# Second embedding's products inside the last expert, its gate's first chunk loaded ahead

## The chip, the core and the metric

The kernel runs on one core of a Trainium2 chip. The number is the device time of one launch in microseconds, the median of three runs. Five engines work side by side, each with its own queue that is worked off in order: PE (TensorE, matrix products), DVE (VectorE), ACT (ScalarE), POOL (GpSimd) and SP, which here issues the DMA transfers of the weights. They wait for one another through semaphores.

## What is computed

Two transformer blocks follow each other on 256 tokens of 1024 channels. The first block has two layers: a differential attention with a short convolution and a dense SwiGLU, then a gated convolution mixer with a mixture of experts (top 2 of 8). Each layer ends with a gated embedding, which is what the change is about. The second block (two layers of four attention mixers with an adaptive norm) only matters by its first product, which takes the output of the first block. Cut to what the change touches:

```python
def moe_swiglu(h, router_w, w1, w3, w2):
    logits = jnp.einsum('nd,de->ne', xt, router_w)
    top_val, top_idx = lax.top_k(logits, TOP_K)            # 2 of 8 experts per token
    gates = jax.nn.softmax(top_val, axis=-1)
    ...                                                    # rows sorted by expert
    return (jax.nn.silu(xb @ w1[e]) * (xb @ w3[e])) @ w2[e]   # summed with gates

for i in range(DEPTH):                                     # DEPTH = 2
    ...                                                    # mixer of the layer
    h = h + swiglu(rms_norm(h, ln_ffn[i]), ...)            # i = 0
    h = h + moe_swiglu(rms_norm(h, ln_ffn[i]), ...)        # i = 1
    gate = jax.nn.sigmoid(rms_norm(h, ln_ple[i]) @ ple_gate[i])   # 1024 x 1024
    h = h + gate * (p[i] @ ple_proj[i])                    # p[i]: 256 x 256
```

The product `p[i] @ ple_proj[i]` doesn't depend on `h`; the gate does.

## The kernel before

**Layout.** `h` stays in SBUF as `hT`, 128 partitions by eight groups of 128 channels by 256 tokens. Products of fp32 numbers are made of three faster ones: each operand is split into `hi` and `lo` (`xhi`, `xlo` for the activations, `pThi`, `pTlo` for the embedding), and hi by hi, hi by lo and lo by hi are added up in PSUM. ACT makes `hi`, then DVE makes `lo`, half a chunk at a time.

**Weights.** All weights come in one stream of chunks of 1 MB in the order of `stream()` (line 77); a chunk is two halves, so `raw3230` is half 0 of chunk 323. SP issues them (line 310) as buffers come free, `pump()` (351) and `get()` (358) decide when a chunk is split and handed out, and at most `look` split chunks are kept ahead (`may_split()`, 344). The first three experts are split like the rest. The last five are "plain": their chunks are used as fp32 without a split, for fewer tokens each, and need neither ACT nor DVE. Two more pairs of raw buffers (`more_raw`, 2106) are open during part of the first block; `i_raw2` bounds the chunks that may use them.

**Order.** A scheduler sets the order on each engine from the order of the program and from pools and priorities; the lists below are its result.

**The gated embedding.** `ple(l)` (810) loads `pT[l]` into `pt`, splits it, makes the products `pps` of the embedding (`ple_proj`, 797: 48 matmuls, copied by ACT into `pp`), and then runs over four chunks of the gate's weights: product `pg` (48 matmuls each), scaled by the norm's factor into `sg`, a sigmoid on ACT, times `pp`, added to `hT`. The norm's factor comes from squares of `hT` (ACT), their sums (POOL, DVE), `ssq` on PE, `rqt` on ACT, small operations on DVE, `rsp` on PE and `nr` on ACT. With each finished pair of groups the next norm's input (`xhi`, `xlo`) is made. It runs twice, after the dense SwiGLU (l = 0) and after the experts (l = 1).

**The end of the experts.** For each of the last five experts `up` makes `H` (line 1434), ACT and DVE gate it into `mg`, `gTp` transposes it, `down` makes `Ys` (1497), and `combine_plain` (1524) scales `Ys` on ACT into `ys`, spreads it to the tokens with a selection matrix (`sc` on PE) and adds it to `hT` on DVE, which also starts `xhi` and `xlo` for the embedding. In `stream()` the last expert's down chunks come first, then `ple_proj` of layer 1 (chunk 330 before the change), then four gate chunks, then `c0` of the second block. `cw1k`, `pt` and other small tables are loaded by the ACT queue.

**The router.** `slots` (1307) makes the selection matrices `S` from the tokens' places; those of the plain experts are six DVE operations (line 1317) among the others.

## Time and profile before

| | us |
|---|---|
| median of 3 runs | 1873.13 |
| lowest, highest | 1872.68, 1876.75 |
| profiled execution | 1875.38 |
| its span | 1873.6 |

PE is the busiest engine; the first three experts keep it busy without a gap, the last five are fed by DMA at its full rate, and the gated embeddings lie on both sides of the experts and of the mixer before them. Times in the rows below are from the span's start. A row of a timeline has start and duration in us, the engine, the line of the kernel, the operation, output and inputs with their shape, how many instructions are taken together (x16), and in brackets how long the engine had stood idle before and what it waited for.

### The profile page before, as it was taken

How to read it: one execution, taken by the hardware profiler on the slowest of the kernel's cores; microseconds unless marked ns; L12 is line 12 of the kernel's file. 1: busy time of each engine (PE TensorE's matmuls, PEld its weight loads, DVE VectorE, ACT ScalarE, POOL GpSimd, SP SyncE). 2: the span in 40 equal slices, each digit the busy share in tenths (PEclk: the TensorE clock that was granted, in tenths of full speed). 3: DMA queues.
4: the chain of work that ended last, by engine and by line, in shares of the span. 5: the costliest groups of instructions: out<-in, count | busy, mean ns of one | idle time of the engine just before them, and what ended most of it. 6: DMA issues, size and time to landing. Idle time of an engine off the chain costs nothing.

```text
span 1873.6 us, 31611 instructions
## 1 busy us (share of the span) xinstructions
PE 1768.3 (94%) x11889; PEld 1428.9 (76%) x11889; DVE 1176.8 (63%) x2150; ACT 909.2 (49%) x1428; POOL 53.0 (3%) x93
## 2 busy tenths in 40 slices
PE   7999999999999999899898888999999999999998
PEld 7989999997888888333232223887899998889997
DVE  7888888687899988101000011886888877666554
ACT  6754435666787866000000002666555456666553
POOL 1000000000000000000000000200000000000000
PEclk9999999998999999999999999999999999999999
DMA  8479886575899989999999999443588864326651
GB/s 308 144 261 315 309 308 218 185 246 210 297 361 330 368 299 326 376 413 412 413 412 413 412 413 383 163 155 106 209 307 303 314 215 138 113 69 204 190 185 53
DMA packets 138544, 508.55 MB, mean 271 GB/s; under 512 B 18192, under 2 KB 18832, under 8 KB 137872
## 3 DMA queue, kind: packets, MB, share of 16 engines
q1 hardware_dynamic: 132480, 496.92, 73.0%
q10 hardware_dynamic: 5904, 9.53, 1.6%
q8 instruction: 96, 1.57, 0.3%
q14 instruction: 64, 0.52, 0.1%
HBM read 505.34 MB, written 1.05 MB: 270 GB/s over the span
## 4 chain that ended last, share of the span: by engine, by line
PE 31%; DMA 22%; DVE 4%; ACT 2%; issue 1%; SPq 0%; DVEq 0%; ACTq 0%
DMA raw<-in_moe_dram 19%; PE y L632 8%; PE up L406 7%; PE zp L406 5%; DMA adaw<-in_ada_dram 2%; PE H L1434 2%; PE S L1839 2%; DVE lo L326 1%; PE op L406 1%; PE pTp L1045 1%; PE cmh L1946 1%; PE oT L1873 1%; ACT hi L325 1%; DVE adacc L865 1%; PE op L431 1%
## 5 line engine op out<-in xcount | busy, mean ns | idle before, releaser
L326 DVE TENSOR_TENSOR lo<-raw,hi 128x1024 fp32r<-128x1024 f32 x516 | 621.8, 1223 | 131.5 <-ACT hi L325 130.0
L325 ACT ACTIVATE hi<-raw 128x1024 fp32r<-128x1024 f32 x516 | 530.9, 1054 | 185.6 <-PE H L1417 38.2
L1434 PE MATMUL H<-raw,xs 128*64 128x512 f32 (+1 forms) x960 | 229.7, 567 | 39.3 <-DMA raw<-in_moe_dram 32.7
L1434 PEld LDWEIGHTS H<-raw,xs 128*64 128x64 f32 x960 | 75.1, 137 | 182.7 <-issue 97.8
L1444 DVE SCALAR_TENSOR_TENSOR mg<-H,gs,mg 128x512 f32<-128x512 f32 (+3 forms) x38 | 26.3, 692 | 290.1 <-PE H L1434 198.7
L632 PE MATMUL y<-ghi,hi 128*128 128x256 f32 x688 | 193.6, 283 | 3.9 <-ACT ghi L377 3.7
L632 PE MATMUL y<-ghi,lo 128*128 128x256 f32 x688 | 194.0, 282 | 2.0 <-DVE lo L326 2.0
L632 PE MATMUL y<-glo,hi 128*128 128x256 f32 x688 | 194.0, 282 | 1.9 <-DVE glo L378 1.9
L1417 PE MATMUL H<-hi,xg 128*128 128x512 f32 (+1 forms) x576 | 178.1, 382 | 0.0
L1443 ACT ACTIVATE mg<-H,gs 128x512 f32<-128x512 f32 (+3 forms) x38 | 24.2, 636 | 307.0 <-PE H L1434 306.9
L865 DVE SCALAR_TENSOR_TENSOR adacc<-adaw,cact,adacc 128x768 f32<-128x768 f32 x126 | 130.9, 1039 | 47.7 <-DMA adaw<-in_ada_dram 46.0
L406 PE MATMUL up<-xhi,hi 128*128 128x258 f32 x480 | 136.3, 284 | 0.2 <-ACT hi L325 0.2
L406 PE MATMUL up<-xhi,lo 128*128 128x258 f32 x480 | 135.6, 283 | 0.0
L406 PE MATMUL up<-xlo,hi 128*128 128x258 f32 x480 | 135.4, 282 | 0.0
L632 PEld LDWEIGHTS y<-ghi,hi 128*128 128x128 f32 x688 | 129.9, 189 | 5.0 <-ACT ghi L377 4.9
L632 PEld LDWEIGHTS y<-glo,hi 128*128 128x128 f32 x688 | 130.3, 189 | 2.9 <-DVE glo L378 2.9
L632 PEld LDWEIGHTS y<-ghi,lo 128*128 128x128 f32 x688 | 130.2, 189 | 2.6 <-DVE lo L326 2.6
L1497 PE MATMUL Ys<-raw,gts 128*64 128x512 f32 x440 | 119.4, 606 | 8.6 <-DMA raw<-in_moe_dram 7.1
L1417 PEld LDWEIGHTS H<-hi,xg 128*128 128x128 f32 x576 | 105.9, 189 | 20.7
L1417 PE MATMUL H<-lo,xg 128*128 128x512 f32 (+1 forms) x288 | 108.9, 378 | 0.0
L406 PE MATMUL H<-xhi,lo 128*128 128x256 f32 x336 | 94.7, 282 | 0.0
L406 PE MATMUL H<-xhi,hi 128*128 128x256 f32 x336 | 94.3, 281 | 0.0
(604 smaller groups left out, 3820.2 us busy)
## 6 DMA issues: line engine op xcount, KB each, us to landing
raw<-in_moe_dram SPq DMA_DIRECT2D x524, 512.0 KB, 10.0
raw<-in_stream_dram SPq DMA_DIRECT2D x316, 512.0 KB, 4.5
adaw<-in_ada_dram SPq DMA_DIRECT2D x64, 768.0 KB, 6.4
cw1k<-in_cw1k_dram ACTq DMA_DIRECT2D x2, 1024.0 KB, 6.4
cw1v<-in_cw1v_dram ACTq DMA_DIRECT2D x2, 1024.0 KB, 5.5
raw<-in_stream_dram SPq DMA_DIRECT2D x4, 472.0 KB, 4.5
hT<-in_xT_dram SPq DMA_DIRECT2D x4, 256.0 KB, 7.2
raw<-in_stream_dram ACTq DMA_DIRECT2D x2, 512.0 KB, 7.6
```

The costliest lines, as they stand in the source:

```text
L325: self.halved = (nc.scalar.activation(hi, raw, AF.Copy), nc.vector.tensor_sub(lo, raw, hi.bitcast(F32)))
L326: nc.vector.tensor_sub(lo, raw, hi.bitcast(F32)))
L406: nc.tensor.matmul(ps, p[:, k, j:j + m], q[:, k, :], start=start and n == 0, stop=n == 3 * nk - 1, skip_group_check=True)
L431: nc.tensor.matmul(ps, p[:, k, c:c + m[n]], q[:, k, :], start=k == i == 0 and not (n and shared), stop=k == KD - 1 and i == 2, skip_group_ ...
L632: self.nc.tensor.matmul(ps, p[:, k, 128 * dt:128 * dt + 128], q[:, k, :], start=f == 0 and n == 0 and dt % 2 == 0, stop=last and n == 5, s ...
L865: nc.vector.scalar_tensor_tensor(acc, w[:, j], self.cact[:, k:k + 1], acc, op0=OP.mult, op1=OP.add)
L1417: nc.tensor.matmul(ps[:, :n], g[s][:, m // 3], w[:, k], start=m == 0, stop=m == 23, skip_group_check=True)
L1434: nc.tensor.matmul(ps[64 * q:64 * q + 64, :c], g[:, k], x[:, kk], start=k == 0, stop=k == KD - 1, skip_group_check=True)
L1443: nc.scalar.activation(t[z, :c], H[0][z, :c], AF.Silu, scale=gs[z, 1:2])
L1444: nc.vector.scalar_tensor_tensor(t[z, :c], H[1][z, :c], gs[z, 1:2], t[z, :c], op0=OP.mult, op1=OP.mult)
L1497: nc.tensor.matmul(Y[e][64 * q:64 * q + 64], gt[:, kk, 64 * n:64 * n + 64], w[:, k, 512 * q:512 * q + 512], start=key[2] == 0 and kk == 0, ...
L1839: nc.tensor.matmul(S[n][:, c:c + b], q[n][:, a:a + 128], k[n][:, 0:b], start=True, stop=True)
```

## The change

1. `stream()`: the embedding's chunk of layer 1 goes ahead of the last expert's last down chunks, right behind its up chunks, and gate chunk 0 between two of these down chunks. So the embedding's chunk is now chunk 323, gate chunk 0 is chunk 328, and the down chunks end with 331.
2. `ple_in`: loading and splitting `pt` is taken out of `ple`. For layer 0 it is done during the feed-forward's phase, its buffers in a pool around it; for layer 1 when the last expert begins.
3. `ple_proj(1)` is called inside the experts' loop behind the last `up`; `ple_proj(0)` at the start of `ple(0)`.
4. `hush`: from the moment that gate chunk 0 is handed out until the last combination is written down, nothing is split; afterwards `hold` ties later splits to the last `xlo`.
5. `ple(1)` has no phase of its own: it runs in that of the experts, with their `mg` buffers for `sg` and their buffers for one of its squares. The two extra pairs of raw buffers may now serve chunks up to `c0`.
6. The selection matrices of the plain experts take a buffer (`yl`) that is used by a combination before.

```diff
--- before.py
+++ after.py
@@ -113,12 +113,17 @@
     for e, f in moe_steps():
         down = down_keys(*prev) if prev else []
         up = up_keys("m1", e, f) + up_keys("m3", e, f)
-        ch += [(k, shapes[k[0], k[2], k[3]], None) for k in (down + up if (e, f) == (NL, 0) else up + down)]
+        last = (e, f) == moe_steps()[-1]
+        a, b = (down, up) if (e, f) == (NL, 0) else (up, down)
+        ch += [(k, shapes[k[0], k[2], k[3]], None) for k in a]
+        if last:
+            rows(("pple", 1), "ple_proj", (1,), 0)
+        ch += [(k, shapes[k[0], k[2], k[3]], None) for k in b]
         prev = e, f
-    ch += [(k, shapes[k[0], k[2], k[3]], None) for k in down_keys(*prev)]
-    rows(("pple", 1), "ple_proj", (1,), 0)
     for i in range(4):
         cols(("gple", 1, i), "ple_gate", (1,), 256 * i)
+        if i == 0:
+            ch += [(k, shapes[k[0], k[2], k[3]], None) for k in down_keys(*prev)]
     for l in range(2):
         for n, parts in enumerate((
                 [(512, 128), (704, 128)], [(640, 64), (832, 32), (1504, 12), (384, 128)], [(0, 256)],
@@ -266,7 +271,8 @@
         self.i_load = self.i_split = self.i_get = 0
         self.raws, self.parts = {}, {}
         self.homes, self.at_home, self.extra, self.got = [], {}, [], []
-        self.i_raw2 = self.at_key["pple", 1]
+        self.i_raw2 = self.at_key["c0", 0]
+        self.hush = False
 
         self.i_three = self.at_key[down_keys(NL - 1, 5)[-1]]
 
@@ -343,6 +349,8 @@
 
     def may_split(self):
 
+        if self.hush:
+            return False
         if self.i_split not in self.raws or self.plain(self.i_split):
             return self.i_split in self.raws
         return len([i for i in self.parts if not self.plain(i)]) < self.look and \
@@ -494,7 +502,7 @@
         h = self.hT[:, 2 * i:2 * i + 2]
         if self.final is not None:
             return self.out_pair(i, h)
-        self.prep_x(i, h)
+        self.last_x = self.prep_x(i, h)
         self.prep_r(i, h, late=self.rows is not False)
 
     def prep_x(self, i, h):
@@ -513,7 +521,11 @@
         if i == 0:
             self.sqs = []
         for n in range(1 if g2 is None else 2):
-            sq = (self.p_ph if n else self.p_s).tile([128, 2, T], F32, tag=f"sq{n}", name="sq", bufs=3)
+            if n:
+
+                sq = self.p_ph.tile([128, 2, T], F32, tag="gth" if i else "gtl", name="sq", bufs=2)
+            else:
+                sq = self.p_s.tile([128, 2, T], F32, tag="sq0", name="sq", bufs=3)
             if n:
                 for j in range(2):
                     k = 2 * i + j
@@ -659,7 +671,7 @@
         self.p_lo = self.pool("lo", 2 * self.look + 2)
         for pool, tag in ((self.p_hi, "hi"), (self.p_lo, "lo")):
 
-            self.home(pool, self.look + 1, tag, lambda i: self.i_get > self.i_three + 1 and i < self.i_raw2 - 6)
+            self.home(pool, self.look + 1, tag, lambda i: self.i_get > self.i_three + 1 and i < self.at_key["pple", 1] - 6)
             self.homes[-1]["all"] = self.look + 1
         self.p_s = self.pool("small", 2)
         self.p_x = self.pool("x", 4)
@@ -794,11 +806,17 @@
         nc.vector.tensor_sub(t1, u[0], u[1])
         nc.vector.tensor_add(t2, u[2], u[3])
 
+    def ple_in(self, l, tile):
+
+        pt = tile("pt", F32)
+        self.nc.scalar.dma_start(pt, self.a["pT"][l])
+        self.pt = tile("pThi", F32R), tile("pTlo", F32R)
+        yield
+        self.hilo(*self.pt, pt)
+
     def ple_proj(self, l):
-        nc, a = self.nc, self.a
-        pt, hi, lo = self.pt
+        hi, lo = self.pt
         w = self.get(("pple", l))
-        self.hilo(hi, lo, pt)
         pp = self.big("pp", [128, KD, T])
         for i in range(4):
             ps = self.ac("pps", (128, 2, T))
@@ -807,17 +825,13 @@
             self.nc.scalar.activation(pp[:, 2 * i:2 * i + 2], ps, AF.Copy)
         return pp
 
-    def ple(self, l, nxt):
-        nc = self.nc
-        p = self.p_ph
-        pt = p.tile([128, 2, T], F32, name="pt")
-        nc.scalar.dma_start(pt, self.a["pT"][l])
-        self.pt = (pt, p.tile([128, 2, T], F32R, name="pThi"), p.tile([128, 2, T], F32R, name="pTlo"))
-        pp = self.ple_proj(l)
+    def ple(self, l, nxt, pp, w=None, tag="sg"):
+        nc = self.nc
         x = self.nx[0:2]
         for i in range(4):
-            w = self.get(("gple", l, i))
-            if i == 3:
+            if i or w is None:
+                w = self.get(("gple", l, i))
+            if i in (0, 3):
                 self.pump()
             ps = self.mm("pg", (128, 2, T))
             if i:
@@ -827,7 +841,7 @@
                 self.mmT2([ps[:, 0], ps[:, 1]], w, x, (0, 128))
                 self.get_r()
                 self.begin_x(*nxt)
-            sg = self.p_ph.tile([128, 2, T], F32, tag="sg", name="sg", bufs=2)
+            sg = self.p_ph.tile([128, 2, T], F32, tag=tag, name="sg", bufs=2)
             self.scaled(sg, ps)
             nc.scalar.activation(sg, sg, AF.Sigmoid)
             nc.vector.tensor_mul(sg, sg, pp[:, 2 * i:2 * i + 2])
@@ -1305,7 +1319,7 @@
 
 
         def slots(es, off=0, plain=False):
-            S = p.tile([128, 2, len(es), 128], F32R, tag="ST" if off else "Ss" if plain else "S", name="S",
+            S = p.tile([128, 2, len(es), 128], F32R, tag="ST" if off else "yl" if plain else "S", name="S",
                        bufs=2 if off else 1)
             for n, e in enumerate(es):
                 for b in range(2):
@@ -1555,7 +1569,16 @@
                     pass
                 self.moe_rest(xtk, cni, slots, slotsT, ghl[0])
                 prev = None
+            if (e, f) == (NE - 1, 0):
+                self.late_consts()
+                pt = self.ple_in(1, lambda nm, dt: p.tile([128, 2, T], dt, tag="yl" if nm == "pt" else "gtl", name=nm,
+                                                          bufs=1 if nm == "pt" else 2))
+                next(pt)
+            if (e, f) == (NE - 1, 1):
+                list(pt)
             up(e, f, prev)
+            if (e, f) == steps[-1]:
+                pp = self.ple_proj(1)
             if e < NL and f == 1:
                 self.add(gather(e + 1) if e < NL - 1 else gather_plain())
             if prev:
@@ -1563,11 +1586,17 @@
                 if f == 0:
                     self.add((combine if e <= NL else combine_plain)(e - 1))
             prev = e, f
+        w = self.get(("gple", 1, 0))
+
+        self.hush = True
         gtrans(*prev)
         down(*prev)
         self.drain()
         for _ in combine_plain(NE - 1):
             pass
+        self.hush = False
+        self.hold = self.last_x
+        return pp, w
 
     def moe_rest(self, xtk, cni, slots, slotsT, ghl):
 
@@ -2062,12 +2091,14 @@
         self.ffn(16, up, lambda f: ("dn", l, f),
                  lambda: self.mod_in(1, 0) if l == 0 else None, self.mod[l][:, 40:48])
 
-    def ffn1(self):
+    def ffn1(self, pt):
         nc = self.nc
         x = self.nx[0:2]
 
         def up(f):
             H = []
+            if f == 2:
+                list(pt)
             for nm in ("f1", "f3"):
                 w = self.get((nm, f))
                 ps = self.mm("H", (128, 2, T))
@@ -2124,11 +2155,14 @@
         self.dump("h1", self.hT)
         with self.tc.tile_pool(name="ada0", bufs=2, reuse_waits="tile") as pool:
             self.adas = self.ada(pool, 0)
-            with self.phase("ffn", 1):
-                self.ffn1()
-            self.dump("h2", self.hT)
-            with self.phase("ple0", 1):
-                self.ple(0, (self.col("ln_mix", 1),))
+            with self.tc.tile_pool(name="pt0", bufs=1, reuse_waits="tile") as p0:
+                with self.phase("ffn", 1):
+                    pt = self.ple_in(0, lambda nm, dt: p0.tile([128, 2, T], dt, name=nm))
+                    next(pt)
+                    self.ffn1(pt)
+                self.dump("h2", self.hT)
+                with self.phase("ple0", 1):
+                    self.ple(0, (self.col("ln_mix", 1),), self.ple_proj(0))
             self.dump("h3", self.hT)
             raw2 = self.more_raw("raw2", "right", 2)
             raw2.__enter__()
@@ -2140,12 +2174,8 @@
                 self.mods(32)
         self.dump("h4", self.hT)
         with self.more_raw("raw3", "left", 2), self.phase("moe", 1, Y=2, ac=2):
-            self.moe((self.col("ln_ple", 1),))
+            self.ple(1, self.mod_in(0, 0) + (self.col("final_norm"),), *self.moe((self.col("ln_ple", 1),)), tag="mg")
         raw2.__exit__(None, None, None)
-        self.dump("h5", self.hT)
-        with self.phase("ple1", 1):
-            self.late_consts()
-            self.ple(1, self.mod_in(0, 0) + (self.col("final_norm"),))
         for l in range(2):
             with self.phase(f"m{l}", 2, S=1, oT=1, ac=2):
                 x = self.mix2(l)

```

DVE in the first gated embedding, from the first split of gate chunk 1 on (51 is gate chunk 1 of layer 0, 52 and 53 the next two). Before:

```order
L326 TENSOR_TENSOR lo_4030<-raw510_3688,hi_4029 128x1024
L386 TENSOR_SCALAR rqm_3996<-ssq_3991 128x2
L393 RECIPROCAL rqy_3999<-rqt_3995 128x2
L326 TENSOR_TENSOR lo_4034<-raw511_3689,hi_4033 128x1024
L378 TENSOR_TENSOR pTlo_3882<-pt_3879,pThi_3881 128x512
L394 SCALAR_TENSOR_TENSOR rqt_3995<-rqy_3999 128x2
L326 TENSOR_TENSOR lo_4042<-raw520_3766,hi_4041 128x1024
L395 TENSOR_TENSOR rqt_3995<-rqt_3995,rqm_3996 128x2
L326 TENSOR_TENSOR lo_4046<-raw521_3767,hi_4045 128x1024
L396 SCALAR_TENSOR_TENSOR rcol_3994<-rqt_3995,rqy_3999 128x2
L576 TENSOR_SCALAR diag_4004<-ident_114,rcol_3994 128x128 x2
L326 TENSOR_TENSOR lo_4119<-raw530_3778,hi_4118 128x1024
```

After:

```order
L332 TENSOR_TENSOR lo_3946<-raw510_3697,hi_3945 128x1024
L332 TENSOR_TENSOR lo_3950<-raw511_3698,hi_3949 128x1024
L332 TENSOR_TENSOR lo_3958<-raw520_3775,hi_3957 128x1024
L332 TENSOR_TENSOR lo_3962<-raw521_3776,hi_3961 128x1024
L332 TENSOR_TENSOR lo_4122<-raw530_3787,hi_4121 128x1024
L394 TENSOR_SCALAR rqm_4023<-ssq_4018 128x2
L401 RECIPROCAL rqy_4026<-rqt_4022 128x2
L332 TENSOR_TENSOR lo_4126<-raw531_3788,hi_4125 128x1024
L402 SCALAR_TENSOR_TENSOR rqt_4022<-rqy_4026 128x2
L403 TENSOR_TENSOR rqt_4022<-rqt_4022,rqm_4023 128x2
L404 SCALAR_TENSOR_TENSOR rcol_4021<-rqt_4022,rqy_4026 128x2
L588 TENSOR_SCALAR diag_4031<-ident_114,rcol_4021 128x128 x2
```

The split of `pt` is gone from this place, and five splits stand ahead of the first small operation (`rqm`), where one did.

PE at the end of the last expert, around its last `H`. Before:

```order
L1434 MATMUL H_14203<-raw3221_14124,xs_7762 64x512
L1434 MATMUL H_14203<-raw3211_14096,xs_7762 64x256
L1434 MATMUL H_14203<-raw3221_14124,xs_7762 64x512
L1434 MATMUL H_14203<-raw3211_14096,xs_7762 64x256
L1497 MATMUL Ys_14150<-raw3230_14127,gts_14197 64x512 x2
L1497 MATMUL Ys_14150<-raw3231_14128,gts_14197 64x512 x2
L1464 MATMUL gTp_14277<-ident_114,mg_14228 128x128 x2
```

After:

```order
L414 MATMUL pps_14331<-pThi_14028,hi_14236 128x256
L414 MATMUL pps_14331<-pTlo_14029,hi_14236 128x256
L414 MATMUL pps_14345<-pThi_14028,hi_14236 128x256
L414 MATMUL pps_14345<-pTlo_14029,hi_14236 128x256
L414 MATMUL pps_14331<-pThi_14028,lo_14237 128x256
L414 MATMUL pps_14345<-pThi_14028,lo_14237 128x256
L414 MATMUL pps_14331<-pThi_14028,hi_14240 128x256
L414 MATMUL pps_14331<-pTlo_14029,hi_14240 128x256
L414 MATMUL pps_14345<-pThi_14028,hi_14240 128x256
L414 MATMUL pps_14345<-pTlo_14029,hi_14240 128x256
L1511 MATMUL Ys_14211<-raw3240_14244,gts_14278 64x512
L414 MATMUL pps_14331<-pThi_14028,lo_14241 128x256
```

Behind the last `H` stood `Ys`, `gTp` and `Ys` of the down chunks; now the 48 `pps` stand there, and the eleventh needs `lo_14241`, the second half's `lo` of chunk 323.

DVE at the end of the experts, from the last copies of `gTp` to the squares of the norm (`hT<-hT,sc` are the four additions of the combination). Before:

```order
L378 TENSOR_TENSOR pTlo_14436<-pt_14433,pThi_14435 128x512
L1540 TENSOR_TENSOR hT_85<-hT_85,sc_14303 128x512
L1540 TENSOR_TENSOR hT_85<-hT_85,sc_14304 128x512
L1540 TENSOR_TENSOR hT_85<-hT_85,sc_14319 128x512
L1540 TENSOR_TENSOR hT_85<-hT_85,sc_14320 128x512
L326 TENSOR_TENSOR lo_14238<-raw3300_14224,hi_14237 128x1024
L326 TENSOR_TENSOR lo_14242<-raw3301_14225,hi_14241 128x1024
L326 TENSOR_TENSOR lo_14250<-raw3310_14245,hi_14249 128x1024
L326 TENSOR_TENSOR lo_14254<-raw3311_14246,hi_14253 128x1024
L506 SCALAR_TENSOR_TENSOR xlo_14312<-hT_85,sv_sb_90,xhi_14311 128x256 x8
L530 TENSOR_TENSOR sq_14346<-sq_14346 128x256
```

After:

```order
L332 TENSOR_TENSOR lo_14314<-raw3280_14301,hi_14313 128x1024
L332 TENSOR_TENSOR lo_14318<-raw3281_14302,hi_14317 128x1024
L332 TENSOR_TENSOR lo_14396<-raw3320_14391,hi_14395 128x1024
L1554 TENSOR_TENSOR hT_85<-hT_85,sc_14453 128x512
L332 TENSOR_TENSOR lo_14400<-raw3321_14392,hi_14399 128x1024
L1554 TENSOR_TENSOR hT_85<-hT_85,sc_14454 128x512
L514 SCALAR_TENSOR_TENSOR xlo_14462<-hT_85,sv_sb_90,xhi_14461 128x256 x2
L1554 TENSOR_TENSOR hT_85<-hT_85,sc_14469 128x512
L1554 TENSOR_TENSOR hT_85<-hT_85,sc_14470 128x512
L514 SCALAR_TENSOR_TENSOR xlo_14462<-hT_85,sv_sb_90,xhi_14461 128x256 x4
L386 TENSOR_TENSOR xlo_14581<-mod0_449,xhi_14580 128x8
L514 SCALAR_TENSOR_TENSOR xlo_14462<-hT_85,sv_sb_90,xhi_14461 128x256 x2
```

Before, four splits (embedding's chunk and gate chunk 0) stood between the additions and `xlo`; now two splits of gate chunk 1 stand among the additions, and those of gate chunk 0 ahead of them.

## Rows read from the trace of the kernel before

**Rows 1.** Page: costliest groups (busy us, mean ns, idle) and the chain by engine.

```profile
PE 31%; DMA 22%; DVE 4%; ACT 2%; issue 1%; SPq 0%; DVEq 0%; ACTq 0%
...
L326 DVE TENSOR_TENSOR lo<-raw,hi 128x1024 fp32r<-128x1024 f32 x516 | 621.8, 1223 | 131.5 <-ACT hi L325 130.0
L325 ACT ACTIVATE hi<-raw 128x1024 fp32r<-128x1024 f32 x516 | 530.9, 1054 | 185.6 <-PE H L1417 38.2
```

**Rows 2.** Timeline of PE, last expert.

```profile
1145.13 0.59 PE L1434 MATMUL H<-raw,xs 128*64 128x512 f32 x1
...
1148.00 3.90 PE L1497 MATMUL Ys<-raw,gts 128*64 128x512 f32 x16
...
1157.15 2.25 PE L1497 MATMUL Ys<-raw,gts 128*64 128x512 f32 x8 [0.25 <-DMA raw<-in_moe_dram]
1159.60 1.08 PE L1497 MATMUL Ys<-raw,gts 128*64 128x512 f32 x4 [0.19 <-DMA raw<-in_moe_dram]
1161.42 1.08 PE L1497 MATMUL Ys<-raw,gts 128*64 128x512 f32 x4 [0.74 <-DMA raw<-in_moe_dram]
```

**Rows 3.** Timeline of PE, combination and second gated embedding.

```profile
1167.85 0.36 PE L406 MATMUL pps<-pThi,hi 128*128 128x256 f32 x1 [0.87 <-DVE hT L1540]
...
1173.69 0.28 PE L431 MATMUL pg<-xhi,hi 128*128 128x256 f32 x1
...
1180.60 0.50 PE L548 MATMUL ssq<-ones,sq 128*128 128x1 f32 x4
...
1183.66 0.38 PE L406 MATMUL pg<-xhi,lo 128*128 128x256 f32 x1 [0.75 <-DVE lo L326]
```

**Rows 4.** Timeline of DVE, the same stretch.

```profile
1166.42 1.29 DVE L1540 TENSOR_TENSOR hT<-hT,sc 128x512 f32<-128x512 f32 x2 [0.62 <-PE sc L1537]
1167.62 5.73 DVE L326 TENSOR_TENSOR lo<-raw,hi 128x1024 fp32r<-128x1024 f32 x4
1173.27 4.75 DVE L506 SCALAR_TENSOR_TENSOR xlo<-hT,sv_sb,xhi 128x256 fp32r<-128x256 f32 x8
```

**Rows 5.** First gated embedding: timeline of PE, of DVE, and DVE busy (its instructions).

```profile
320.31 0.58 PE L548 MATMUL ssq<-ones,sq 128*128 128x1 f32 x4
...
352.75 0.39 PE L443 MATMUL cv<-hi,xhi 128*128 128x256 f32 x1 [2.17 <-ACT xhi L505]
...
315.50 3.79 DVE L506 SCALAR_TENSOR_TENSOR xlo<-hT,sv_sb,xhi 128x256 fp32r<-128x256 f32 x4
...
330.33 1.23 DVE L326 TENSOR_TENSOR lo<-raw,hi 128x1024 fp32r<-128x1024 f32 x1 [3.34 <-ACT hi L325]
...
351.46 0.69 DVE L835 TENSOR_TENSOR hT<-hT,sg 128x512 f32<-128x512 f32 x1
...
330.33:352.15 21.82, 21.03 (x27) 1.00 0.58 181
```

**Rows 6.** Windows: length, busy by engine, PE clock granted, DMA share, GB/s.

```profile
core 0: us, PE busy (x) PEld busy (x) DVE busy (x) ACT busy (x) POOL busy (x), PEclk, DMA share, GB/s
350.00:354.00 4.00, 1.82 (x12) 1.61 (x11) 3.97 (x7) 2.06 (x5) 0.88 (x1) 0.87 0.62 177
354.00:356.00 2.00, 2.00 (x11) 2.00 (x11) 0.95 (x4) 1.11 (x2) 0.00 (x0) 0.50 0.95 326
...
1160.00:1168.00 8.00, 4.76 (x25) 2.27 (x22) 3.56 (x6) 5.80 (x8) 0.00 (x0) 1.00 0.92 339
1210.00:1216.00 6.00, 5.68 (x27) 5.39 (x26) 1.92 (x11) 0.49 (x2) 0.00 (x0) 0.50 0.00 0
```

**Rows 7.** Timeline at the router: PE and DVE.

```profile
435.74 7.10 PE L1358 MATMUL xgp<-S,xtk 128*128 128x128 f32 x32 [2.29 <-DVE S L1321]
...
436.39 0.27 DVE L1317 TENSOR_SCALAR S<-io,rkp 128x128 fp32r<-128x128 f32 x1
```

**Rows 8.** Window in the stage of expert 2, columns as in rows 6.

```profile
660.00:680.00 20.00, 20.00 (x106) 16.96 (x105) 19.27 (x22) 13.61 (x17) 0.00 (x0) 1.00 0.92 321
```

**Rows 9.** Timeline of POOL, second gated embedding.

```profile
1170.28 4.21 POOL L526 TENSOR_TENSOR sq<-sq 128x512 f32<-128x512 f32 x2 [407.57 <-ACT sq L522]
```

## The prediction

> **What bounds the kernel now.** I read the page's chain first [rows 1]: 31% of the span runs over PE and 22% over DMA. So at each place that the change touches I asked which of the two ends last there, and who waits for whom in the gaps. I read three places engine by engine.
>
> *The end of the experts.* Down chunks come half by half: eight `Ys` for two halves start at 1157.15, the next at 1159.60, so 1.23 us for each, with PE waiting for DMA each time; the last half comes 1.82 us after the one before, and `Ys` ends at 1161.42 + 1.08 = 1162.50 [rows 2]. DMA bounds here. Then a chain of small steps follows, `ys`, `sc`, additions to `hT` until 1166.42 + 1.29 = 1167.71, and only then do the 48 `pps` run, from 1167.85 to the first `pg` at 1173.69 [rows 3, 4]. In their shadow DVE makes four splits and eight `xlo` (to 1178.02) [rows 4]. So the product of the embedding costs PE 5.8 us, but it also covers DVE's work ahead of the gate; the first `pg` start as soon as the last `pps` is done. That cover is what the change takes away.
>
> *The first gated embedding.* DVE waits 3.34 us for a split whose `hi` stands behind copies of `pps` on ACT; from 330.33 to the last addition (351.46 + 0.69 = 352.15) it hardly rests. PE runs dry and waits 2.17 us for `xhi`, and its granted clock is 0.50, the lower level (1.2 GHz), from 354 to 356 [rows 5, 6].
>
> *The router.* The 32 `xgp` wait 2.29 us for DVE's small `S` operations [rows 7].
>
> **Part by part.** The profiled execution took 1875.38 us, 2.25 over the median of 1873.13; sums are made against the profiled one and carried over to the median.
>
> 1. *First embedding: products ahead, `pt` already there.* The split of `pt` leaves ACT and DVE; the 48 `pps` now stand inside `pg0` on PE, their copies ahead of the splits on ACT, so DVE makes five splits without the long wait. On PE `pg0` now ends 48 x 0.12 = 5.7 us later, and so does `ssq`: 320.31 + 5.6 = 325.9 [rows 5]. `rqt` comes behind six splits on ACT (about 327.2); the small operations, one split and the transposed factor take some 3.6 us more, so the first `sg` starts near 330.8, where before it follows the split at 330.33, near 331.5 [rows 5]. From 330.33 to the last addition before has eight splits, now six behind the first `sg`. DVE is busy 21.03 us in that stretch [rows 5]; less two splits of 1.22 [rows 1] that is 18.6; from 330.8 and with 0.6 us of waits it ends at 350.0, so `xhi` comes some 2.0 us sooner. PE, with the same work, runs dry about when it did and waits about 1 us for `xhi` instead of 2.17. I take **-2.0 us**. Bounds: 0 (copies and splits wait for one another in a new place) and -4.4 (the whole 2.17 and the 0.7 of waits that PE has before its own last stretch vanish, and the slow clock with them, 0.13 x 4 + 0.50 x 2 = 1.5 us of full clock [rows 6]).
>
> 2. *`S` for the last five experts made later.* Six operations of 0.27 us leave DVE's queue in the router; two or three stand there between others that `xgp` and its casts need, and PE is past its wait by then: **-0.3** (0 to -0.8) [rows 7]. They now stand behind a combination near 671 us, where DVE is busy 19.27 of 20 us and PE all of it [rows 8]: 1.6 us more for a queue with 0.73 to spare, though its splits run ahead by several chunks: **+0.3** (0 to +1.6).
>
> 3. *`pt` early.* 256 KB beside the stream cost it 1.82 - 1.23 = 0.6 us [rows 2]; where `pt` goes now for the first embedding, the attention's projection, PE has work: **+0.1** (0 to +0.6). At the end of the experts the stream gains those 0.6 us back.
>
> 4. *Last expert.* Two chunks, four halves, are loaded ahead of the last down chunks, which so land 4 x 1.23 - 0.6 = 4.3 us later: DMA alone would let `Ys` end near 1166.8. On PE the last `H` (ends at 1145.72 [rows 2]) is followed by the 48 `pps`, and these need splits of a chunk that lands only then. ACT and DVE have nothing else there but `mg`: two `hi` of 1.05, then two `lo` of 1.22 [rows 1] behind the `mg`, the second done near 1150.1. Some ten `pps` can go before, so PE stands about 2.5 us, and `pps` end at 1150.1 + 38 x 0.117 = 1154.6. Then 54 `Ys` at 0.244 (16 in 3.90 [rows 2]) and `gTp`, 0.7: 1168.4. So PE ends the phase and no longer DMA; between 1166.8 and 1169.4 I take **1168.3, 5.8 us later than before**. cw1k's 1 MB now goes out beside the last halves; `pt` is the one row of such a transfer beside a full stream, and four times its 0.6 us is 2.4, most of it behind the last down half: +0.3 (0 to 2.4), inside the range given.
>
> 5. *Combination and gate.* Before, additions end 5.2 us after `Ys`. Now the two `lo` of gate chunk 1 stand among them, 2.44 us, about half in time in which DVE waited anyway (0.62 and more ahead of each pair [rows 4]): 1168.3 + 5.2 + 1.3 = 1174.8, the first two `xlo` among them. Eight `xlo` take 4.75 [rows 4], so the last is done near 1179.5, and `pg0` follows by a few matmuls, 1180.2 to 1180.7; before it ended at 1180.6 [rows 3]. The 5.8 us of `pps` and the splits of gate chunk 0 leave this stretch, and the 5.8 us by which the experts end later take their place: **0.0**. POOL's sums of squares (2.1 us each [rows 9]) move with `xhi` to about 1177 to 1181.5, so `ssq` comes at 1181 to 1182.5 instead of 1180.60: +0.9; the 0.75 us that the next `pg` waited for `lo` [rows 3] goes. `nr` stands behind more `hi`, so the first `sg` starts 2 to 3.5 us later, but no splits stand behind it any more, and later additions are within 1.5 us of before on either side. The last `xlo` of this stretch moves by -1.5 to +2.0; I take **+0.3**.
>
> Sum: -2.0 - 0.3 + 0.3 + 0.1 + 0.0 + 0.3 = -1.6: 1873.8 for the profiled execution and **1871.5** as median, no change that can be told.
>
> DVE and POOL slow each other here: four `xlo` took 3.79 us beside POOL's sums [rows 5], where four of eight at 4.75 [rows 4] would take 2.4, so 1.4 more. The Trainium skill (SBUF — State Buffer, "Who interferes with whom") states that a DVE instruction with two SBUF inputs and a GpSimd instruction that reads SBUF exclude each other for the whole instruction; the rows agree that they interfere, not by how much. This speaks against the change, which leaves only `xlo` for POOL's sums to fall on. Were both sums (4.2 us) to hold up `xlo` in full instead of 1.4, the total would be +1.2 and the time 1874.3, inside the forecast's bound; my sum goes by the row.
>
> **Rivals.**
> *(a) Faster, 1867.* The waits really go: the first embedding gives 4.4 (PE stands less and the clock stays at 2.4 GHz), the router 0.5, the seam 1.5, in sum about -6.4. For: DVE's 3.34 us wait has a plain cause that the new order removes, and these places are chains of waits, not of work. Against: at the seam the 4.3 us of moved DMA and the wait of PE for `lo` eat what the moved `pps` give.
> *(b) Slower, 1877.* TensorE's clock at the seam. From 1168.3 to 1174.5 PE would have only the 16 `sc`. Before, with the same `sc` in it, 4.76 us busy in the 8 from 1160 kept the clock at 1.00, but 1.82 in the 4 from 350 were followed by 0.50, and from 1210 it stayed at 0.50 for 6 us with PE busy [rows 6]. There 27 matmuls took 5.68 us, 0.21 each; at that, instead of 0.12, the 96 matmuls of `pg0` and `pg1` lose 0.09 each, 8.6 us if all run so. It decides from about 60 of them: +5.4, which with -1.6 makes +3.8.
>
> The Trainium skill (TensorE: Matmul & The Clock Gate, "What's actually happening") says that the chip lowers the clock to 1.2 GHz when the engine has been idle and gives 2.4 GHz back after it has worked for some time. The rows at 354 agree; by that rule a fall at the seam would cost one stretch like that one, +1.5, and the time would be 1873.0, inside the forecast's bound.
>
> *(c) No change, 1873.* The change doesn't take the products out of the way, it only pushes the experts: if the splits of the moved chunk come later still (ACT or DVE behind `mg`), `Ys` ends at 1169.4 and everything behind it 1.1 later, in sum -0.5.
>
> **How the numbers follow.** A measurement of this kernel tells 0.2%, 3.75 us. The forecast and (c), both within it, have 0.56; (a) and its neighbours with a sum below -3.75 have 0.30; (b) has 0.14. The range goes from 1866.5, just past (a), to 1876.5: the slow ends of terms 1 to 3 add 2 + 0.3 + 1.3 + 0.5 = 4.1 and that of 5 another 1.7, and more than +5.0 of it together, or (b), is left out, as is what lies below (a).
>
> **What would show it.** `Ys` ending 1167 to 1169.5 on before's clock, `pps` with a wait for `lo` of about 2.5 us, `pg0` within 1 us of 1180.6; DVE's 3.34 us wait gone and the last `xhi` of the first embedding 2 us earlier. Wrong: `Ys` ending after 1170 (the wait for `lo` longer, or DMA short of buffers); a granted clock under 1 between 1170 and 1188 (b); none under 1 at 350 to 357 (a); a new wait of PE for DVE near 671 us (term 2).

## The result and the profile after

The kernel after takes 1883.02 us (median of 6 runs, 1879.54 to 1885.42); the kernel before took 1872.45 us beside it (6 runs, 1867.87 to 1876.75). The ratio is 1.0053, with an interval of 1.0035 to 1.0071: slower by about 10 us, where 1871.5 and no change had been forecast. The profiled execution after has a span of 1883.5 us, that of before 1873.6.

The page's two costliest groups of the splits stand as in [rows 1] (busy us, mean ns, idle):

```profile
L332 DVE TENSOR_TENSOR lo<-raw,hi 128x1024 fp32r<-128x1024 f32 x516 | 620.5, 1221 | 135.7 <-ACT hi L331 134.1
L331 ACT ACTIVATE hi<-raw 128x1024 fp32r<-128x1024 f32 x516 | 530.9, 1054 | 197.6 <-PE y L644 37.8
```

As many of them, each as long as before, and both pages count 11889 matmuls on PE: no work was added. (PE's busy time is 7 us longer, 1775.5 after and 1768.3 before, at a mean granted clock of 0.980 against 0.984.) So the 10 us come from waits and from what follows them. To find them I cut both spans at five places that both programs have: the last `gTp` of expert 2 (the last expert with a router in front of it), the end of the last expert's last `H`, the end of its last `Ys`, the first `ssq` of the second gated embedding, and the first `hT<-hT,sv_sb,nr` of the stage behind that embedding. All are rows of the timelines of PE and DVE (start plus duration where an end is meant). In us, with the experiments below in the same table:

```
kernel                          to gTp   to H end  to Ys end  to ssq  to hT,nr  to the end   span
before                          748.1     397.6      16.8      18.1     36.9      656.1     1873.6
after                           747.3     408.2      21.7      18.3     35.7      652.3     1883.5
pt_behind_branch                748.2     399.3      21.7      18.3     36.3      653.9     1877.7
before_plus_load                749.2     408.1      16.1      19.4     34.9      653.9     1881.5
hush_earlier                    744.6     399.2      21.7      11.4     37.4      650.9     1865.2
hush_earlier, again             748.6     401.0      21.7      11.4     37.3      650.4     1870.4
products_behind                 746.2     398.7      16.3      22.3     36.7      649.1     1869.3
first_embedding_only            746.5     398.0      16.8      18.4     34.9      653.9     1868.5
products_ahead_of_last_up       748.6     401.3      18.8      11.4     35.4      651.1     1866.5
gate_chunk_behind_down          750.6     403.0      17.3      15.1     35.2      649.9     1871.1
```

The first and the last column spread over 6 to 7 us between profiles, the first by 4 us where the kernel is the same (744.6 and 748.6), so nothing small is read from them. The two in which after stands out are the second, +10.6 us, and the fourth, in which the prediction had counted on 5 us less than before and got 0.2 more.

**The second column.** Ahead of the five plain experts stands a branch (`moe_rest`'s overflow path, not taken here). A name that ends in q, as in SPq, is the queue part of an engine, which works off branches, semaphores and the issues of DMA. The waits of SP's queue and the instructions of the branch's line, before (L1577):

```profile
SPq L1577 <- SPq L1577: 4.7, 2, 4.5
...
L1577 SPq EVENT_SEMAPHORE  x8: 17/17/17, 750.1 to 750.8; - x8
...
L1577 SPq COMPARE_BRANCH  x1: 53/53/53, 745.6 to 745.6; - x1
```

and after (L1606), with the one transfer that ACT issues there (a waits row gives the total, the times, and the longest wait; a row of the line gives min/median/max in ns and the first and last start):

```profile
SPq L1606 <- SPq L1606: 14.2, 1, 14.2
...
L1606 SPq EVENT_SEMAPHORE  x8: 17/17/17, 759.0 to 759.6; - x8
...
L1606 SPq COMPARE_BRANCH  x1: 53/53/53, 744.8 to 744.8; - x1
...
L1606 ACTq COMPARE_BRANCH  x1: 54/54/54, 756.5 to 756.5; - x1
...
755.53 0.33 ACTq L812 DMA_DIRECT2D pt<-in_pT_dram  x1
...
pt<-in_pT_dram ACTq DMA_DIRECT2D x1, 256.0 KB, 3.5
```

Where the branch's body is left out, SP runs through eight semaphore waits. The program counts finished transfers on eight semaphores, here called lanes, and each of these waits is for everything that was issued on its lane ahead of the branch, by any engine. The scheduler had placed the load of `pt` for the second embedding on ACT ahead of ACT's own branch. Its buffer (tag `yl`) comes free only with the combination of expert 2, so it went out at 755.53 and landed 3.5 us later, at 759.0. SP had come to the branch at 744.8 and stood until then. What that does to the weights, in windows of 4 us, after (length, PE busy, granted clock, DMA share, GB/s):

```profile
744.00:748.00 4.00, 3.62 (x17) 1.00 1.03 412
748.00:752.00 4.00, 3.53 (x14) 1.00 0.11 41
752.00:756.00 4.00, 2.67 (x14) 1.00 0.00 0
756.00:760.00 4.00, 0.82 (x2) 0.82 0.27 78
```

and before:

```profile
744.00:748.00 4.00, 4.00 (x19) 1.00 1.00 346
748.00:752.00 4.00, 3.41 (x15) 1.00 0.26 101
752.00:756.00 4.00, 2.91 (x16) 1.00 0.90 290
```

The stream of weights rests some 9 us longer, and the five plain experts behind it take as long as their weights take, so nothing makes up for it.

**The last expert and the combination.** PE after, which answers [rows 2, 3]:

```profile
1157.58 0.50 PE L414 MATMUL pps<-pThi,lo 128*128 128x256 f32 x2 [1.41 <-DVE lo L332]
...
1170.97 6.23 PE L1511 MATMUL Ys<-raw,gts 128*64 128x512 f32 x28
1178.04 1.14 PE L1551 MATMUL sc<-ST,ys 64*128 64x256 f32 x8 [0.85 <-ACT ys L1543]
...
1180.85 1.18 PE L1551 MATMUL sc<-ST,ys 64*128 64x256 f32 x4 [1.67 <-DVE hT L1554]
...
1184.37 0.58 PE L439 MATMUL pg<-xhi,hi 128*128 128x256 f32 x1 [2.34 <-ACT xhi L513]
...
1195.51 0.50 PE L560 MATMUL ssq<-ones,sq 128*128 128x1 f32 x4
```

`Ys` now runs without a wait for DMA, as the prediction said, and ends 21.7 us behind the last `H` instead of 16.8. But behind it PE waits for an addition and for `xhi`. DVE after in that stretch, which answers [rows 4], and under it the split on ACT that it waits for:

```profile
1178.97 1.22 DVE L332 TENSOR_TENSOR lo<-raw,hi 128x1024 fp32r<-128x1024 f32 x1 [5.00 <-ACT hi L331]
1180.11 0.68 DVE L1554 TENSOR_TENSOR hT<-hT,sc 128x512 f32<-128x512 f32 x1
1183.95 1.23 DVE L332 TENSOR_TENSOR lo<-raw,hi 128x1024 fp32r<-128x1024 f32 x1 [3.16 <-ACT hi L331]
1185.09 0.68 DVE L1554 TENSOR_TENSOR hT<-hT,sc 128x512 f32<-128x512 f32 x1
...
1188.54 4.20 DVE L514 SCALAR_TENSOR_TENSOR xlo<-hT,sv_sb,xhi 128x256 fp32r<-128x256 f32 x4
...
1182.86 1.06 ACT L331 ACTIVATE hi<-raw 128x1024 fp32r<-128x1024 f32 x1 [3.93 <-DMA raw<-in_stream_dram]
```

The two `lo` of gate chunk 1 stand in DVE's order ahead of the first and of the second addition. The second of them waits for an `hi` that waits for its weights, and the additions, `xhi` and the gate wait behind it. In windows after (columns as above) the granted clock then falls to the lower level, 1.2 GHz:

```profile
1177.00:1180.00 3.00, 1.33 (x10) 1.00 0.92 296
1180.00:1183.00 3.00, 1.18 (x4) 0.80 1.01 407
1183.00:1186.00 3.00, 1.18 (x4) 0.50 1.02 419
1186.00:1189.00 3.00, 3.00 (x9) 0.50 1.02 416
1189.00:1192.00 3.00, 3.00 (x16) 0.50 0.57 228
```

**The first gated embedding** after, DVE and PE, which answers [rows 5]:

```profile
312.13 1.28 DVE L605 TENSOR_TENSOR hT<-hT,y 128x512 f32<-128x512 f32 x2
...
331.41 0.69 DVE L598 TENSOR_TENSOR sg<-pg,nr 128x512 f32<-128x512 f32 x1 [1.09 <-ACT nr L591]
...
350.57 0.69 DVE L849 TENSOR_TENSOR hT<-hT,sg 128x512 f32<-128x512 f32 x1
...
326.05 0.50 PE L560 MATMUL ssq<-ones,sq 128*128 128x1 f32 x4
...
351.86 0.38 PE L451 MATMUL cv<-hi,xhi 128*128 128x256 f32 x1 [2.34 <-ACT xhi L513]
```

The wait of 3.34 us is gone. From the start of the first `hT<-hT,y` to that of the last `hT<-hT,sg` it is 350.57 - 312.13 = 38.44 us; before it was 351.46 - 311.45 = 40.01, with this first row (the last is in [rows 5]):

```profile
311.45 1.28 DVE L593 TENSOR_TENSOR hT<-hT,y 128x512 f32<-128x512 f32 x2
```

### The profile page after: what moved, and what is told of

Its sections match the earlier page's. It is cut to its first block, busy times and chain, and to the rows that moved or that the text cites. A ratio compares the mean times of both kernels' runs of the same rounds, so it can differ in the third digit from the quotient of the medians.

```text
span 1883.5 us, 31601 instructions
## 1 busy us (share of the span) xinstructions
PE 1775.5 (94%) x11889; PEld 1432.3 (76%) x11889; DVE 1179.2 (63%) x2150; ACT 909.5 (48%) x1428; POOL 53.2 (3%) x93
## 5 line engine op out<-in xcount | busy, mean ns | idle before, releaser
L1448 PE MATMUL H<-raw,xs 128*64 128x512 f32 (+1 forms) x960 | 234.4, 574 | 42.3 <-DMA raw<-in_moe_dram 38.4
```

Source lines behind the costliest of these rows:

```text
L1448: nc.tensor.matmul(ps[64 * q:64 * q + 64, :c], g[:, k], x[:, kk], start=k == 0, stop=k == KD - 1, skip_group_check=True)
```

## The experiments

The theory (A): two things made the loss, one that the sum did not have and one that it had too small. The stall of SP at the branch costs some 9 us; the two `lo` among the additions cost more than the half-hidden 2.44 us of the prediction. Its rivals: that the loss at the branch is PE's (a wait for code behind it), that the moved products (pps) set the end, and that the first embedding gives nothing to the total.

**The load of `pt` behind the branch.** The kernel after, with that load held until an instruction of the plain experts:

```
-                nc.scalar.activation(t[z, :c], H[0][z, :c], AF.Silu, scale=gs[z, 1:2])
+                self.last_mg = nc.scalar.activation(t[z, :c], H[0][z, :c], AF.Silu, scale=gs[z, 1:2])
...
-                next(pt)
+                with self.after(self.last_mg):
+                    next(pt)
```

> The changed kernel with one edit: the load of pt for the second embedding is held until the last mg of expert 6, so it stands behind the branch of the router's overflow case on ACT instead of ahead of it. Theory A (SP stands at that branch until every DMA issued before it has landed, and pt, whose buffer comes free only at 755.5 us, was one of them): SP's eight semaphore operations behind the branch come at 750 to 751 us as before the change (759.0 to 759.6 in the changed kernel), DMA's gap between 748 and 760 shrinks from about 11 us to about 3, and the kernel gets 8 to 9 us faster than the changed one, 1874 +- 2 median. Theory B (the loss is all at the seam behind the last expert, where H ends late for other reasons): no change, 1883. Theory C (SP's 14.2 us are the loading of its code behind the branch and vary with the program's layout): the stall stays anywhere from 4 to 14 us and has nothing to do with pt.

Measured: 1876.59 us (10 runs), beside 1870.47 of before (31 runs): ratio 1.0024 (1.0005 to 1.0042). The waits and the branch of this kernel:

```profile
SPq L1607 <- SPq L1607: 5.2, 3, 3.5
...
L1607 SPq EVENT_SEMAPHORE  x8: 17/17/17, 749.1 to 751.3; - x8
...
L1607 PEldq COMPARE_BRANCH  x1: 6243/6243/6243, 756.2 to 756.2; - x1
```

The stall goes back to the size of before, and the second column from 408.2 to 399.3. By the ratios 0.29% of 1871, 5.4 us, are gone, less than the 8 to 9 expected; the ends of the two intervals allow anything between nothing and 12.

**The same load in the kernel before.** Nothing else is changed, and nothing reads the tile:

```
+            if (e, f) == (NE - 1, 0):
+                t = p.tile([128, 2, T], F32, tag="yl", name="pt2", bufs=1)
+                nc.scalar.dma_start(t, self.a["pT"][1])
             up(e, f, prev)
```

> The kernel before the change with one edit: a second load of the same 256 KB, used by nobody, into the buffer yl, issued on ACT ahead of the branch, so it waits for the last reader of yl. Theory A: SP's stall at the branch grows from 4.5 to about 14 us and the kernel gets 8 to 9 us slower, 1881 +- 2. Theory B and C: the 256 KB cost 0.6 us at most, 1873.

Measured: 1878.68 us (10 runs), ratio 1.0042 (1.0025 to 1.0059), 7.9 us more than before (8 to 9 were expected). The waits of SP and its branch in this kernel:

```profile
SPq L1580 <- SPq L1580: 14.6, 1, 14.6
...
L1580 SPq EVENT_SEMAPHORE  x8: 17/17/17, 761.2 to 761.8; - x8
...
L1580 PEldq COMPARE_BRANCH  x1: 4003/4003/4003, 757.2 to 757.2; - x1
```

The second column is 408.1, as after. So one load of 256 KB that nobody needs makes the kernel before slower by most of what the change cost, and the cause is shown from both sides; its price in the total lies between 5.4 and 7.9 us by these two runs, with wide intervals. PE's own part of the branch takes 4.0 us here against 6.2 in the kernel with the load behind the branch, so it falls where the time grows; it is not the cause.

**No gate chunk split among the additions.** The kernel with the late load, and in it the splits held from the embedding's products on instead of from the first gate chunk on:

```
             if (e, f) == steps[-1]:
+                self.hush = True
                 pp = self.ple_proj(1)
...
         w = self.get(("gple", 1, 0))
-
-        self.hush = True
```

> e1 with splits stopped already before the second embedding's products, so that gate chunk 1 is not split among the additions of the last combination but after the last xlo. In the changed kernel DVE waited 3.16 us there for the hi of its second half. Theory D (that wait is what the seam loses): the last xlo of the combination comes 3 to 5 us sooner than in e1, the next pg product waits 1 to 2 us more for its split, in all 2 to 3 us faster than e1, 1871. Theory E (the seam is bound by PE and the small chain, the split is hidden): within 1 us of e1.

Measured: 1869.46 us (10 runs), ratio 0.9992 (0.9977 to 1.0008), and in the runs beside the kernel with the products ahead (below) 0.9991. DVE in the profile of these later runs:

```profile
1173.35 1.29 DVE L1554 TENSOR_TENSOR hT<-hT,sc 128x512 f32<-128x512 f32 x2 [5.25 <-PE sc L1551]
...
1175.41 1.28 DVE L1554 TENSOR_TENSOR hT<-hT,sc 128x512 f32<-128x512 f32 x2
...
1182.19 0.43 DVE L543 TENSOR_TENSOR sq<-sq 128x256 f32<-128x256 f32 x1
```

From `Ys` to `ssq` it is 11.4 us instead of 18.3: 6.9 gained where 2 to 3 had been expected, and by the ratios (1.0024 to 0.9992) 0.32%, 6.0 us. The granted clock, too, stays at 1.00 there: from 1171 to 1210 no window of 3 us is below.

**The second embedding back in its place.** The kernel with the late load, but products, stream order and splits of the second embedding as in the kernel before:

```
-        if last:
-            rows(("pple", 1), "ple_proj", (1,), 0)
...
-            if (e, f) == steps[-1]:
-                pp = self.ple_proj(1)
...
-            self.ple(1, self.mod_in(0, 0) + (self.col("final_norm"),), *self.moe((self.col("ln_ple", 1),)), tag="mg")
+            self.moe((self.col("ln_ple", 1),))
+            self.ple(1, self.mod_in(0, 0) + (self.col("final_norm"),), self.ple_proj(1), tag="mg")
```

> e1 with the stream's order and the place of the second embedding's products as before the change (behind the last combination), no stop of splits; what is left of the change is the first embedding's order, pt early, the shared buffers. Theory D': the seam change alone costs about 5 us (in the changed kernel the distance from the last H to the last xlo before c0 grew by 5.0 us more than the start of H), so 1869 to 1870, 4 to 5 us faster than e1. Theory F (the prediction's: the seam is neutral): within 1 us of e1, 1873 to 1874.

Measured: 1871.62 us (10 runs), ratio 1.0012 (0.9995 to 1.0029), by the ratios 2.2 us below the kernel with the late load and between the two expectations. This tells little: with `pt` split early the scheduler put PE's first gate products ahead of half of `pps`, PE waited for `xlo`, and `Ys` to `ssq` took 22.3 us against 18.1 before. It is not the kernel before's embedding that was put back, but a third order.

**The first embedding alone.** The kernel before with only that part of the change:

```
+    def ple_in(self, l, tile):
...
-            if i == 3:
+            if i == 3 or first and i == 0:
...
+            if f == 2:
+                list(pt)
...
-                    self.ple(0, (self.col("ln_mix", 1),))
+                    self.ple(0, (self.col("ln_mix", 1),), self.ple_proj(0))
```

> The kernel before with the change to the first embedding alone: pT[0] loaded and split during the first FFN, its products ahead of the router weights, and one addition batch pumped a step earlier; the second embedding stays as in the kernel before. Theory A (the stall at the branch and the two lo tiles at the seam made the whole loss): this part gives what the sum gave it, the four xlo splits of the first embedding no longer stand behind a 3.34 us wait and cv of the first embedding ends 1.5 to 2 us earlier against the first addition of its stage; the time is 0.998 to 1.000 of the kernel before, some 1868.5 to 1870.5 against 1870.5. Theory G (what the front gains is taken back by the router or by the clock at the router's start): the last product of the first embedding ends earlier but the last gTp of expert 2 is not earlier than 748 us, and the ratio is 1.000 or above.

Measured: 1869.57 us (12 runs) beside 1870.87 of before (35 runs): ratio 0.9988 (0.9973 to 1.0004). DVE of this kernel at the two ends of the stage:

```profile
313.03 1.28 DVE L593 TENSOR_TENSOR hT<-hT,y 128x512 f32<-128x512 f32 x2
...
351.45 0.69 DVE L845 TENSOR_TENSOR hT<-hT,sg 128x512 f32<-128x512 f32 x1
```

38.42 us, 1.59 less than before, as theory A has it. The last `gTp` of expert 2 comes at 746.5, but that column is too uneven to decide against theory G, and the interval still holds no change at all: that this part gives something to the total is not shown.

**The products into PE's waits.** The kernel of the earlier hush, with the embedding's chunk streamed ahead of the last `up` chunks and the products called ahead of that step:

```
+        if last:
+            rows(("pple", 1), "ple_proj", (1,), 0)
         ch += [(k, shapes[k[0], k[2], k[3]], None) for k in a]
-        if last:
-            rows(("pple", 1), "ple_proj", (1,), 0)
...
+            if (e, f) == steps[-1]:
+                self.hush = True
+                pp = self.ple_proj(1)
             up(e, f, prev)
```

> The kernel with the late pT load and the early hush, and in it the embedding's weight chunk streamed ahead of the last expert's last up chunks, with its products called ahead of that up step. Theory H (the products pps, some 5 us of TensorE, stand between the last H and Ys and set the end of the phase): they go into TensorE's waits for weights, last H end to Ys end falls from 21.7 to 17 or 18 us, and the time is 3 to 4 us below the run of the same kernel without this, 0.998 of it. Theory I (the scheduler lays part of pps behind the last H anyway, and the last up chunks land 1 us later because 0.5 MB stands ahead of them): last H end to Ys end falls by 2.5 us at most, the last H end is later by as much as was gained, and the ratio between the two stays 0.999 to 1.001.

and its base again on the same chip:

> The kernel with the late pT load and the early hush again, on this chip, as the base of the two runs beside it: by the run before, 0.9992 of the kernel before (0.9977 to 1.0008), so 0.998 to 1.001 of it here; Ys end to first ssq 11 to 12 us.

Measured: 1867.53 us (12 runs), ratio 0.9983 (0.9971 to 0.9996); the base 1869.05 us (12 runs), 0.9991 (0.9979 to 1.0004). PE of the kernel with the products ahead:

```profile
1131.60 0.38 PE L414 MATMUL pps<-pThi,hi 128*128 128x256 f32 x1 [1.46 <-ACT hi L331]
...
1150.57 0.39 PE L414 MATMUL pps<-pThi,hi 128*128 128x256 f32 x1 [0.70 <-ACT pp L825]
...
1167.57 1.08 PE L1511 MATMUL Ys<-raw,gts 128*64 128x512 f32 x4 [0.17 <-DMA raw<-in_moe_dram]
```

Half of `pps` goes into PE's waits, half stays behind the last `H`, and the last `Ys` waits for DMA again. `H` to `Ys` is 18.8 instead of 21.7 us, between the two expectations; the time is 1.5 us lower than the base's, which these intervals don't tell from none. Against the kernel before it is 0.17% faster (0.04 to 0.29), the one version here whose interval lies below 1, and so also below the kernel after.

**The first gate chunk back behind the down chunks.** The kernel of the run before, with

```
+    ch += [(k, shapes[k[0], k[2], k[3]], None) for k in down_keys(*prev)]
     for i in range(4):
         cols(("gple", 1, i), "ple_gate", (1,), 256 * i)
-        if i == 0:
-            ch += [(k, shapes[k[0], k[2], k[3]], None) for k in down_keys(*prev)]
```

and the chunk taken behind the last `down` call in the order of the code. A chunk is split when it is taken, held splits or not, so its two `lo` come among the additions.

> The kernel of the run with the products ahead of the last up step, and in it the gate's first chunk streamed behind the last expert's down chunks and not ahead of them. Theory J (the two lo tiles of a gate chunk cost some 6 us where they stand among the combination's additions): Ys end comes 2 to 3 us earlier since the down chunks land earlier, but the first gate chunk's lo tiles now stand among the additions, and the stretch from Ys end to ssq grows by 3 to 6 us: 1 to 4 us slower than the run without this. Theory K (what counted was the wait for the second chunk's data, and a chunk that lands in time costs the additions only its own 2 lo of some 1.2 us each): the stretch grows by 2.5 us at most, and the time is the same or 1 us lower.

Measured: 1868.85 us (12 runs), ratio 0.9990 (0.9976 to 1.0005). DVE of this kernel:

```profile
1172.63 1.23 DVE L331 TENSOR_TENSOR lo<-raw,hi 128x1024 fp32r<-128x1024 f32 x1 [13.28 <-DMA raw<-in_stream_dram]
1173.77 0.68 DVE L1553 TENSOR_TENSOR hT<-hT,sc 128x512 f32<-128x512 f32 x1
1174.37 1.22 DVE L331 TENSOR_TENSOR lo<-raw,hi 128x1024 fp32r<-128x1024 f32 x1
...
1178.33 0.69 DVE L1553 TENSOR_TENSOR hT<-hT,sc 128x512 f32<-128x512 f32 x1 [0.76 <-PE sc L1550]
...
1184.44 0.43 DVE L542 TENSOR_TENSOR sq<-sq 128x256 f32<-128x256 f32 x1
```

Here the two `lo` stand among the additions as they do after, and the second has its data. So the 6.9 us part in two. With the data there, `Ys` to `ssq` is 15.1 us, 3.7 more than without these `lo`; the 18.3 us of the kernel after are another 3.2 more, the size of its wait of 3.16 us. Of the 3.7, DVE's chain from `Ys` to the end of the last `sq` is 1184.87 - 1170.86 = 14.0 us here against 1182.62 - 1171.33 = 11.3 in the earlier hush (the later profile): 2.7. Of this 0.76 is a wait for `sc` ahead of the last addition, which the earlier hush does not have: its four matmuls took 2.05 us here (from 1176.24), the four ahead of them 1.13, as the clock fell. The other 2.0 are the two `lo`, 2.45 us, of which only some 0.5 falls in time in which DVE waited anyway. The last 1.0 of the 3.7 is PE's again: the granted clock fell to 0.50 from 1177 to 1183 here and `ssq`, behind the gate's products, came 1.1 us after the last `sq` instead of 0.15. Both expectations hold half. Theory J has the stretch right (3.7 us for 3 to 6), and the 1.3 us by the ratios lie at the lower end of its 1 to 4, but these intervals don't tell them from none, and the end of `Ys` gained 1.5 us behind the last `H` where 2 to 3 had been expected. Theory K is right that the wait for the data was a part of its own, and too low for what the two `lo` bring with them.

## Why the prediction was wrong

Two steps of the sum failed: term 3, which had no price for a load that stands ahead of the branch, and term 5, which had the two `lo` among the additions too small. Taking them out gave back 0.29% and 0.32%. What is left of 0.53% is -0.08%, the 0.9992 of the earlier hush (0.9991 when it was run again); the forecast's 1871.5 is 0.9991 of 1873.13. That these meet is in part luck: the sum holds 1.3 us for the two `lo`, which the earlier hush doesn't have there, and both intervals hold no change.

- *Term 1, the first embedding: right in its stretch.* -1.6 us for -2.0: 38.42 to 38.85 in the eight profiles that have the new order, 40.01 and 39.98 in the two that don't. `ssq` was predicted for 325.9 and the first `sg` for 330.8; they came at 326.05 and 331.41, in a stage that began 0.7 later. PE's wait for `xhi` did not shrink to 1 us, it is 2.34; the clock fell in after (0.59 and 0.56 from 352 to 356), and in the run with the first embedding alone, which runs the same code there, it stayed at 1.00. Of the eight profiles with the new order it fell there in four, so rival (a)'s condition is luck here, not the change.
- *Term 2, the router: no price seen.* PE's wait for `S` is 2.29 us as in [rows 7], where -0.3 had been taken; at 671 us there is no new wait of PE.
- *Term 3, `pt` early: the first step that failed.* It was priced as 256 KB beside a stream, +0.1, at most +0.6, and for the second embedding as a gain. It was asked where its bytes go, and not what stands behind its issue: the load waits on ACT for a buffer, and the branch makes SP wait for every transfer issued ahead of it. So it cost the stream some 9 us, and the total 5.4 to 7.9 by the two runs on it. The trace of before had shown the place (SP's 4.5 us at L1577), and the program of after has the load on ACT ahead of the branch; the prediction has no row of that place and none of SP's queue.
- *Term 4, the last expert: right in its stretch.* `H` to `Ys` grew by 4.9 us; 1168.3 as the end meant 22.6 us and 21.7 were measured. PE ends the phase. The wait for `lo` was 1.41 us and not 2.5.
- *Term 5, the combination: the second step that failed, in its size.* From `Ys` to `ssq` the prediction had 1181 to 1182.5 less 1168.3, some 13 to 14 us; it was 18.3. Its two `lo` were to cost 1.3 us, half of them hidden. Some 2.0 of their 2.45 us are not hidden, since each stands ahead of an addition that PE, ACT and DVE itself wait for; the second brought a wait for its weights of 3.2 us, and the fall of PE's clock that followed some 1.7. That the moved chunks push the gate's next chunk back on the queue was in term 4 and was not carried on to here.
- *The `xlo` of term 5: too small as well.* Eight took 4.75 us in the sum, and 0.87 + 4.20 + 0.87 = 5.9 after, four of them (at 1188.54) beside POOL's sums. The prediction named this, with 1.4 us, but took the 4.75 as it was; its +1.2 for the worst case counts the 1.4 as if it were in the sum. The 1.4 itself was read too low: of the eight of before one took 1.50 us beside POOL, where the median is 0.47. Two `xlo` without POOL take 0.87 us, so four some 1.7 and not 2.4, and those beside POOL took 2.0 us more at the first embedding and 2.5 here. The earlier hush has this too (5.9), so it is no part of the 6.9 us gained there.
- *Rival (b): its mechanism came, its price not.* The clock was at 0.50 from 1183 to 1192, with some 25 gate products in that time and not 60. It cost about 1.0 us at `ssq`, because DVE's `xlo` and `sq` end only shortly before, and some 0.8 ahead of the last addition, which waited 0.77 us for `sc`. Before and in the earlier hush it stayed at 1.00 in the same stretch. The Trainium skill (TensorE: Matmul & The Clock Gate, "What's actually happening") says that the chip lowers the clock when the engine has been idle; the trace agrees, as PE was busy 1.33 of the 3 us from 1177 and 1.18 of the next 3, in which the clock fell. The idleness came from the `lo` that stood ahead of the additions: without them, in the earlier hush, the clock did not fall.

No rival had the branch. Of what the prediction said would show it wrong, two signs came: `Ys` ended after 1170, at 1177.2, for a reason that was not named, and the granted clock was under 1 between 1170 and 1188, at (b)'s place.

## What to carry to other kernels

When a step is moved, ask for each of its transfers which instruction waits for its semaphore, not only who reads the data: the branch here waits for every transfer issued ahead of it, and a load that waits for a late buffer then holds the whole stream. In a chain of additions look at what stands on the engine's own order ahead of each, and count most of the work put there (2.0 of 2.45 us here), with the wait for its operands. A load that must be early belongs behind the branch, or (not tried here) in a buffer that is free by then.

## What the runs showed of the hardware

SP's stall ended with the landing of a transfer that another engine had issued: 14.2 us at a branch that is not taken, in the trace of after, 14.6 in the kernel before with the spare load. The longest such wait is 3.5 to 5.2 us in the eight profiles in which that load is not ahead. The comparison itself took SP 53 ns.

PE's part of the same branch took 6.1 us before (L1577), 3.5 after (L1606), 6.2 with the late load and 4.0 with the spare load. The Trainium skill (Runtime: NRT & Kernel Launch, "Instruction fetch mechanics") says that a branch out of the fetched window must wait for a new page of code; the traces show the time and fetches of code beside it, not what it waited for. Why it is shorter where the weights rest is open; that it is the free DMA queues was not tried.
